# The transfers of a triangular substitution: from SP's queue, per chunk and block, to GpSimd's queue, per block for both chunks

## The chip, the cores and the metric

The kernel runs on one core of a Trainium2 chip. The metric is the device time of one execution in microseconds (us). Times of the profile count from the start of its span. PE is TensorE, with PEld its weight loads; DVE is VectorE, ACT is ScalarE, POOL is GpSimd and SP is SyncE, which here issues transfers only. SPq and POOLq are the instructions with which these engines issue transfers.

## The reference

A trunk of four pre-norm residual layers works on a sequence of 256 tokens of width 1024: a causal pooling mixer, a gated DeltaNet layer, an attention layer with compressed keys and values, and a pooling mixer again. All is fp32. The change lies in the second layer. Cut to what matters here:

```
proj = h @ w_in                       # q, k, v, gate, beta, decay
qkv = silu(causal_depthwise_conv(qkv, conv_w))
q, k = l2norm(q) * dk**-0.5, l2norm(k)          # 8 heads, dk 128, dv 256
L = where(strict, (k*beta) @ k.T * decay, 0)    # per head and chunk
A = eye(C) + L
sol = triangular_solve(A, [v*beta, k*beta*exp(g)], lower=True)
# then a scan over chunks: v_new = u - w @ state; o = q @ state + attn @ v_new; ...
y = rmsnorm(o) * silu(gate)
out = y.reshape(S, 2048) @ w_out
```

The reference takes chunks of 64 tokens. The kernel takes two chunks of 128, which gives the same output, and so needs the inverse of sixteen unit lower triangular matrices of 128 x 128 (8 heads, 2 chunks).

## The kernel before, in words

**Weights.** Every projection is made with split weights. `weights` (L115 to L130) loads a raw tile of 512 KB, two chunks of 128 rows and 512 columns, on SP's queue; for each chunk ACT rounds it to a high part `whi` (L128) and DVE subtracts that from the raw value for the low part `wlo` (L130). PE then makes three matmuls for each product: high by high, high by low, low by high. There are three raw buffers and nine of each of the parts (the ring). A raw buffer is free for the next load when the subtract of its second chunk has ended.

**Order.** The tile scheduler orders the instructions of all engines by a simulated timeline; what an engine then has in its order it executes in that order, and an instruction that waits holds all behind it on that engine. SP's transfers are such an order too. In the delta-rule layer (`gdn_layer`) PE's order is fixed as written: keys, queries, the gate and values are projected in 512-column pieces, and other steps of the layer are put between the k-chunks of a piece. `keys`, `queries` and `values` end in a convolution (`conv`: ACT scales, L658; DVE adds three taps, L661) and a SiLU on ACT (`kqT` L695, `vc` L816); PE then transposes `vc` (L100, `values_turned`) and ACT scales the result into `vR` (L829).

**The inverse.** `lower` writes `LT` on DVE (L721), one tile a chunk, with all heads. `substitution` (L746 to L779) inverts the 32 x 32 diagonal blocks, 64 in all (two chunks t, eight heads m, four blocks d). It brings them from `LT` to a layout with one block in each of 64 partitions by way of a DRAM buffer `d_l`: eight stores, one for each t and d (L752), and one load `Lb` (L757). On POOL it makes 31 steps of forward substitution (L762 product `pr`, L766 subtract into `Tb`). The result goes back by a buffer `d_t`: one store (L768) and eight loads into `T` (L772), again one for each t and d. All eighteen transfers are on SP's queue, among the raw loads. On POOL other work stands among the steps: the `Gb` product (L795), which needs the queries' `kqT`, and the norms `rq` (L797 to L801).

**What takes `T`.** `inverses` transposes `T` in blocks of 32 on DVE into `U` (L848) and clears parts of `Lb` and `Tb` on POOL (L847). `pairs`, `joined`, `turned`, `whole` and `last` are PE steps that assemble the whole inverse from the blocks; `pairs(0)`, 16 matmuls with `T` and `LT`, is the first of them. They stand in PE's fixed order among the k-chunks of `values(2)`, `values(3)` and `gate(3)`.

The order of the steps, as written (`scored` makes the attention tiles, `key_norms` and `query_norms` the norms):

```
queries(0, [do(lower, 0)], (), (), [do(key_norms, 1), do(lower, 1), substitution])
gate(1)
values(0, [do(query_norms, 0)], [do(scored, 0)])
queries(1, (), (), (), [do(values_turned, 0)])
gate(2)
values(1, [do(query_norms, 1)], [do(scored, 1)])
values(2, (), (), [do(values_turned, 1), inverses], [inv("pairs", 0)])
```

Of the kernel before, what the change touches and what calls it, by code (L numbers as in the profile page):

```python
# [16 lines left out]
P = 128  # L17
D = 1024
S = 256
NT = S // P  # L20
# [22 lines left out]
def trunk(ctx: ExitStack, tc: tile.TileContext, x, positions, norm_g, pool_w_in, pool_w_grp,  # L43
          pool_scale, pool_w_out, gdn_w_in, gdn_conv, gdn_a_log, gdn_dt_bias, gdn_norm_g,
          gdn_w_out, mla_w_in, mla_q_norm_g, mla_w_uq, mla_kv_norm_g, mla_w_ukv, mla_w_out,
          final_g, out, depth=4, final=True):
    nc = tc.nc
# [22 lines left out]
    def big(name, *dims, dt=F32):  # L70
        return s4.tile([P, *dims], dt, tag="s4", name=name)
# [7 lines left out]
    def small(name, *dims, bufs=2):  # L79
        return sm.tile([P, *dims], F32, tag=name, name=name, bufs=bufs)  # L80
# [14 lines left out]
    def matmul(*args, **opts):  # L95
        ins = nc.tensor.matmul(*args, **opts)  # L96
        return tc.keep_in_program_order(ins) if pinned["on"] else ins

    def transpose(*args):
        ins = nc.tensor.transpose(*args)  # L100
        return tc.keep_in_program_order(ins) if pinned["on"] else ins
# [460 lines left out]
    def gdn_layer(i, j, hT):  # L562
        H = GDN_H
# [71 lines left out]
        for t in range(NT):  # L635
            nc.gpsimd.dma_start(
                out=Gb[t].rearrange("p h s -> p (h s)"),
                in_=d_g[t * H:(t + 1) * H, :].rearrange("(a h) s -> a (h s)", a=1).to_broadcast(
                    [P, H * P]))
# [26 lines left out]
        Q, B = 4, 32  # L666
        Tb_ = big("Tb", B, B)
        Tb = Tb_[:M * Q]
        nc.gpsimd.memset(Tb, 0.0)
        nc.gpsimd.memset(Tb.rearrange("m r c -> m (r c)")[:, ::B + 1], 1.0)  # L670
        T = [big("T", H, P) for _ in range(NT)]
        for t in range(NT):
            nc.gpsimd.memset(T[t], 0.0)

# [37 lines left out]
        def against(dst, rhs, sf, hf, t):  # L712

            ps = bank(aux, "aux").rearrange("p (b s) -> p b s", b=4)
            tt = slice(t * P, (t + 1) * P)
            for b in range(4):
                matmul(ps[:, b], lhsT=kT[hf][:, b, tt], rhs=rhs[hf][:, b, tt],
                                 start=True, stop=True)
            for b in range(4):
                h = 4 * hf + b  # L720
                nc.vector.scalar_tensor_tensor(  # L721
                    out=dst[t][:, h, :], in0=ps[:, b], scalar=sf[:, t, h:h + 1],
                    in1=DT[t][:, h, :], op0=ALU.mult, op1=ALU.mult)

        LT = [big("LT", H, P) for _ in range(NT)]

        def keys(hf, *between):
            channels(kT, GDN_QK, hf, 0, between)
# [11 lines left out]
        def lower(hf):  # L740
            for t in range(NT):
                against(LT, kT, s2, hf, t)

        free = []

        def substitution():  # L746

            d_l = dram.tile([M * Q, B * B], F32, name="d_l")
            lv = d_l.rearrange("(t m d) (r c) -> t d r m c", t=NT, d=Q, r=B)
            for t in range(NT):  # L750
                for d in range(Q):
                    nc.sync.dma_start(out=lv[t, d],  # L752
                                      in_=LT[t][d * B:(d + 1) * B, :, d * B:(d + 1) * B])
            Lb_ = big("Lb", B, B)
            Lb = Lb_[:M * Q]
            free.extend((Lb_, Tb_))
            nc.sync.dma_start(out=Lb, in_=d_l.rearrange("m (r c) -> m r c", r=B))  # L757
            pr = small("pr", 256, bufs=1)[:M * Q]
            for r in range(B - 1):
                n, c = B - 1 - r, r + 1  # L760
                pv = pr[:, :n * c].rearrange("m (a b) -> m a b", a=n)
                nc.gpsimd.tensor_tensor(out=pv, op=ALU.mult,  # L762
                                        in0=Lb[:, r, r + 1:, None].to_broadcast([M * Q, n, c]),
                                        in1=Tb[:, r:r + 1, :c].to_broadcast([M * Q, n, c]))
                tv = Tb[:, r + 1:, :c]
                nc.gpsimd.tensor_tensor(out=tv, in0=tv, in1=pv, op=ALU.subtract)  # L766
            d_t = dram.tile([M * Q, B * B], F32, name="d_t")
            nc.sync.dma_start(out=d_t.rearrange("m (r c) -> m r c", r=B), in_=Tb)  # L768
            tv = d_t.rearrange("(t m d) (r c) -> t d r m c", t=NT, d=Q, r=B)
            for t in range(NT):  # L770
                for d in range(Q):
                    nc.sync.dma_start(out=T[t][d * B:(d + 1) * B, :, d * B:(d + 1) * B],  # L772
                                      in_=tv[t, d])
            nc.vector.reciprocal(rki, rk)
            nc.vector.tensor_tensor(out=kds, in0=rk[:, 0, :], in1=DT[0][:, :, P - 1],
                                    op=ALU.mult)
            nc.vector.tensor_scalar(neG, eG[:, 1, :], -1.0, None, ALU.mult)
            nc.gpsimd.tensor_tensor(out=ktok, in0=ktok, op=ALU.mult,
                                    in1=kds[:, :, None].to_broadcast([P, H, P]))  # L779
# [57 lines left out]
        def inverses():  # L837
# [8 lines left out]
            for t in range(NT):  # L846
                nc.gpsimd.memset(X1[t][:, :, 32:64], 0.0)  # L847
                nc.vector.transpose(U[t].rearrange("p m c -> p (m c)"),  # L848
                                    T[t].rearrange("p m c -> p (m c)"))

            def blocks(a, x):
                return a.rearrange("p m (a b c) -> p m a b c", a=2, b=2)[:, :, :, x]
# [3 lines left out]
            def pairs(t):  # L856
                ps = bank(aux, "aux").rearrange("p (m a c) -> p m a c", m=H, a=2)
                for h in range(H):
                    matmul(ps[:, h], lhsT=LT[t][:, h], rhs=blocks(T[t], 0)[:, h],
                           start=True, stop=True)  # L860
# [11 lines left out]
            def u_turned(t):  # L872
                ps = bank(aux, "aux").rearrange("p (m c) -> p m c", m=H)
                for h in range(H):
                    transpose(ps[:64, h], U[t][:64, h, :64], ident[:64, :64])
                nc.scalar.copy(T[t][:64, :, :64], ps[:64])

            def whole(t):
                ps = bank(aux, "aux").rearrange("p (m c) -> p m c", m=H)
                for h in range(H):  # L880
                    matmul(ps[:, h], lhsT=LT[t][:64, h], rhs=T[t][:64, h, :64],
                           start=True, stop=True)
# [179 lines left out]
    def mla_layer(i, j, hT):  # L1062
# [203 lines left out]
        return layer_out(mla_w_out[j], yT, units(POOL_W // P), i)  # L1266

    layers = (pool_layer, gdn_layer, mla_layer)
    setups = [gdn_setup, mla_setup][:max(0, depth - 1)]
    first = cols_of(pool_w_in[0], POOL_W + (len(WINDOWS) - 1) * CW)  # L1270
# [58 lines left out]
```

## Time and profile before

| | |
|---|---|
| median of 3 runs | 872.14 us (871.36 to 873.38) |
| profiled execution | 875.96 us |
| its span | 874.3 us |
| granted TensorE clock, mean | 0.979 |
| the delta-rule layer's stretch 215 to 345 us | PE waits 11.0 us for `vc`, 10.0 us for `kqT` |
| stretch 302 to 334 us | PE busy 21.03 of 32 us |

A row of a timeline has the start, the duration, the engine, the line and what it writes and reads, and in brackets how long the engine was idle before and what released it. A row of the waits has the waiting instruction, the one it waited for, the sum of us, the number of times and the longest. A row of transfers has the KB of one and the us from issue to landing. SP's rows of the timeline show only the issue, not the wait ahead of it.

### The profile page before, as it was taken

How to read it: one execution, taken by the hardware profiler on the slowest of the kernel's cores; microseconds unless marked ns; L12 is line 12 of the kernel's file. 1: busy time of each engine (PE TensorE's matmuls, PEld its weight loads, DVE VectorE, ACT ScalarE, POOL GpSimd, SP SyncE). 2: the span in 40 equal slices, each digit the busy share in tenths (PEclk: the TensorE clock that was granted, in tenths of full speed). 3: DMA queues.
4: the chain of work that ended last, by engine and by line, in shares of the span. 5: the costliest groups of instructions: out<-in, count | busy, mean ns of one | idle time of the engine just before them, and what ended most of it. 6: DMA issues, size and time to landing. Idle time of an engine off the chain costs nothing.

```text
span 874.3 us, 16119 instructions
## 1 busy us (share of the span) xinstructions
PE 839.3 (96%) x5967; PEld 782.2 (89%) x5967; DVE 597.6 (68%) x1142; ACT 490.3 (56%) x1006; POOL 150.2 (17%) x288
## 2 busy tenths in 40 slices
PE   7999999999779959999999999999999999999996
PEld 6999998989769949878988998999989989999986
DVE  5588776467868956556666667767867657767852
ACT  6566655466645534555556564556655566556542
POOL 4010000344119930012121101000000120000012
PEclk8999999999889988999999999999999999999999
DMA  7666656566455543213547776663453547566651
GB/s 237 205 193 194 189 171 218 147 183 204 121 145 150 165 124 108 82 49 121 166 124 209 216 167 169 180 183 97 136 153 98 168 141 218 179 189 193 195 192 49
DMA packets 111288, 140.43 MB, mean 161 GB/s; under 512 B 23340, under 2 KB 53224, under 8 KB 111208
## 3 DMA queue, kind: packets, MB, share of 16 engines
q1 hardware_dynamic: 109056, 138.17, 52.7%
q0 software_dynamic: 320, 1.06, 0.4%
q8 instruction: 47, 0.77, 0.3%
q10 hardware_dynamic: 1832, 0.16, 0.2%
q14 instruction: 33, 0.27, 0.1%
HBM read 137.79 MB, written 1.58 MB: 159 GB/s over the span
## 4 chain that ended last, share of the span: by engine, by line
PE 83%; POOL 7%; DMA 3%; DVE 3%; issue 1%; ACT 1%; SPq 0%; POOLq 0%; ACTq 0%; DVEq 0%
PE acc L96 68%; PE aux L96 12%; PE tp L100 3%; POOL Tb L766 3%; POOL pr L762 2%; DMA raw<-in_gdn_w_in_dram 2%; DMA gain<-in_norm_g_dram 1%; DVE h L329 1%; DVE wlo L130 1%; POOL xr L322 0%; ACT junk L235 0%; DMA Lb<-d_l 0%; POOL rq L683 0%; DVE x L379 0%; DVE cv L661 0%
## 5 line engine op out<-in xcount | busy, mean ns | idle before, releaser
L130 DVE TENSOR_TENSOR wlo<-raw,whi 128x512 fp32r<-128x512 f32 (+1 forms) x495 | 345.7, 719 | 175.0 <-ACT whi L128 168.3
L128 ACT CAST whi<-raw 128x512 fp32r<-128x512 f32 (+1 forms) x508 | 301.8, 618 | 278.9 <-PE acc L96 196.3
L96 PE MATMUL acc<-hTh,whi 128*128 128x256 f32 x832 | 236.3, 285 | 0.0
L96 PE MATMUL acc<-hTl,whi 128*128 128x256 f32 x832 | 235.7, 283 | 0.0
L96 PE MATMUL acc<-hTh,wlo 128*128 128x256 f32 x832 | 234.9, 282 | 0.0
L96 PEld LDWEIGHTS acc<-hTh,whi 128*128 128x128 f32 x832 | 158.4, 190 | 0.7
L96 PEld LDWEIGHTS acc<-hTl,whi 128*128 128x128 f32 x832 | 158.4, 190 | 0.4
L96 PEld LDWEIGHTS acc<-hTh,wlo 128*128 128x128 f32 x832 | 158.3, 190 | 0.1
L96 PE MATMUL acc<-whi,yTh 128*128 128x256 f32 (+1 forms) x384 | 116.7, 322 | 0.0
L96 PE MATMUL acc<-wlo,yTh 128*128 128x256 f32 (+1 forms) x384 | 116.5, 319 | 0.0
L96 PE MATMUL acc<-whi,yTl 128*128 128x256 f32 (+1 forms) x384 | 91.7, 318 | 0.0
L96 PEld LDWEIGHTS acc<-wlo,yTh 128*128 128x128 f32 x384 | 72.1, 188 | 5.0
L96 PEld LDWEIGHTS acc<-whi,yTh 128*128 128x128 f32 x384 | 71.9, 188 | 5.1
L96 PEld LDWEIGHTS acc<-whi,yTl 128*128 128x128 f32 x384 | 63.2, 188 | 5.8
L317 POOL TENSOR_TENSOR hg<-x,gain 128x256 f32<-128x256 f32 x18 | 14.9, 832 | 261.3 <-DVE x L379 256.8
L96 PE MATMUL acc<-whi,hTh 128*128 128x512 f32 (+1 forms) x144 | 56.9, 402 | 0.7 <-ACT hTh L221 0.7
L96 PE MATMUL acc<-wlo,hTh 128*128 128x512 f32 (+1 forms) x144 | 56.8, 397 | 0.5 <-DVE wlo L130 0.3
L96 PE MATMUL acc<-whi,hTl 128*128 128x512 f32 (+1 forms) x144 | 45.7, 390 | 0.0
L96 PEld LDWEIGHTS acc<-whi,hTh 128*128 128x128 f32 x144 | 27.8, 193 | 7.0 <-ACT hTh L221 1.9
L96 PEld LDWEIGHTS acc<-wlo,hTh 128*128 128x128 f32 x144 | 27.8, 193 | 7.0 <-DVE wlo L130 1.8
L461 POOL COPY win<-u 128x4 f32<-128x4 f32 x8 | 2.8, 355 | 175.7 <-ACT u L455 175.7
L96 PEld LDWEIGHTS acc<-whi,hTl 128*128 128x128 f32 x144 | 26.9, 190 | 5.6 <-DVE hTl L226 0.2
(336 smaller groups left out, 1423.2 us busy)
## 6 DMA issues: line engine op xcount, KB each, us to landing
raw<-in_pool_w_in_dram SPq DMA_DIRECT2D x60, 512.0 KB, 4.4
raw<-in_gdn_w_in_dram SPq DMA_DIRECT2D x48, 512.0 KB, 4.2
raw<-in_pool_w_out_dram SPq DMA_DIRECT2D x32, 512.0 KB, 3.7
raw<-in_mla_w_in_dram SPq DMA_DIRECT2D x24, 512.0 KB, 4.5
raw<-in_mla_w_uq_dram SPq DMA_DIRECT2D x36, 256.0 KB, 3.5
raw<-in_pool_w_grp_dram SPq DMA_DIRECT2D x16, 512.0 KB, 3.9
raw<-in_gdn_w_out_dram SPq DMA_DIRECT2D x16, 512.0 KB, 3.4
raw<-in_mla_w_ukv_dram SPq DMA_DIRECT2D x32, 256.0 KB, 3.1
```

The lines of the kernel that those rows point to most:

```text
L96: ins = nc.tensor.matmul(*args, **opts)
L100: ins = nc.tensor.transpose(*args)
L128: a = nc.scalar.copy(hi, v)
L130: b = e.tensor_tensor(out=lo, in0=v, in1=hi.bitcast(F32), op=ALU.subtract)
L317: nc.gpsimd.tensor_tensor(out=self.early[t, a], in0=xs[t][:, sl], in1=self.g[:, sl], op=ALU.mult)
L329: nc.vector.scalar_tensor_tensor(out=h[:, cut:], in0=xs[t][:, sl], scalar=r[:, 0:1], in1=self.g[:, sl], op0=ALU.mult, op1=ALU.mult)
L461: nc.gpsimd.tensor_copy(nxt[:, :, :d], cur[:, :, :d])
L762: nc.gpsimd.tensor_tensor(out=pv, op=ALU.mult, in0=Lb[:, r, r + 1:, None].to_broadcast([M * Q, n, c]), in1=Tb[:, r:r + 1, :c].to_broadcast ...
L766: nc.gpsimd.tensor_tensor(out=tv, in0=tv, in1=pv, op=ALU.subtract)
```

## The change

The eighteen transfers of `substitution` are issued by POOL, not SP. `LT` and `T` become one tile each for both chunks, and the rows of `d_l` and `d_t` are ordered so that one transfer takes a diagonal block d of all heads and both chunks: four stores, `Lb`, `d_t` and four loads, ten in all. Each store or load of a block now moves 32 partitions by 16 runs of 32 numbers (64 KB), where it was 32 by 8 (32 KB). The arithmetic is the same.

```diff
-        T = [big("T", H, P) for _ in range(NT)]
+        Ts = big("T", NT, H, P)
+        T = [Ts[:, t] for t in range(NT)]
+
+        def diagonal(a, d):
+
+            return a[d * B:(d + 1) * B, :, :, d * B:(d + 1) * B].rearrange("p t h c -> p (t h) c")
+
...
-        LT = [big("LT", H, P) for _ in range(NT)]
+        LTs = big("LT", NT, H, P)
+        LT = [LTs[:, t] for t in range(NT)]
...
             d_l = dram.tile([M * Q, B * B], F32, name="d_l")
-            lv = d_l.rearrange("(t m d) (r c) -> t d r m c", t=NT, d=Q, r=B)
-            for t in range(NT):
-                for d in range(Q):
-                    nc.sync.dma_start(out=lv[t, d],
-                                      in_=LT[t][d * B:(d + 1) * B, :, d * B:(d + 1) * B])
+            lv = d_l.rearrange("(m d) (r c) -> d r m c", d=Q, r=B)
+            for d in range(Q):
+                nc.gpsimd.dma_start(out=lv[d], in_=diagonal(LTs, d))
...
-            nc.sync.dma_start(out=Lb, in_=d_l.rearrange("m (r c) -> m r c", r=B))
+            nc.gpsimd.dma_start(out=Lb, in_=d_l.rearrange("m (r c) -> m r c", r=B))
...
             d_t = dram.tile([M * Q, B * B], F32, name="d_t")
-            nc.sync.dma_start(out=d_t.rearrange("m (r c) -> m r c", r=B), in_=Tb)
-            tv = d_t.rearrange("(t m d) (r c) -> t d r m c", t=NT, d=Q, r=B)
-            for t in range(NT):
-                for d in range(Q):
-                    nc.sync.dma_start(out=T[t][d * B:(d + 1) * B, :, d * B:(d + 1) * B],
-                                      in_=tv[t, d])
+            nc.gpsimd.dma_start(out=d_t.rearrange("m (r c) -> m r c", r=B), in_=Tb)
+            tv = d_t.rearrange("(m d) (r c) -> d r m c", d=Q, r=B)
+            for d in range(Q):
+                nc.gpsimd.dma_start(out=diagonal(Ts, d), in_=tv[d])
```

Lines behind the first piece have other numbers in the changed kernel: the stores of `LT` are L758, `Lb` L762, the steps L767 and L771, `d_t` L773, the loads of `T` L776, the `Gb` product L798, the memset of `Tb` L850.

SP's queue in the delta-rule layer, from the middle of the raw loads of the input projection to those of the output projection (rows with - are of before, with + of the change):

```order
-L757 DMA Lb<-d_l 64x1024
-L115 DMA raw<-in_gdn_w_in_dram 128x2x512 x13
-L768 DMA d_t<-Tb 64x1024
-L115 DMA raw<-in_gdn_w_in_dram 128x2x512
-L772 DMA T<-d_t 32x8x32 x5
-L115 DMA raw<-in_gdn_w_in_dram 128x2x512
-L772 DMA T<-d_t 32x8x32 x3
-L115 DMA raw<-in_gdn_w_in_dram 128x2x512 x5
+L115 DMA raw<-in_gdn_w_in_dram 128x2x512 x48
 L115 DMA raw<-in_gdn_w_out_dram 128x2x512 x8
```

Before, three single raw loads stood behind `d_t` and between the loads of `T`; now the 48 raw loads follow each other with nothing between them.

POOL's order in the same layer at the start of the substitution, before (`ktok` is the scaled keys, the row ahead of `Gb`):

```order
L778 TENSOR_TENSOR ktok<-ktok,kds 128x1024
L795 TENSOR_TENSOR Gb<-Gb,kqT 128x512
L762 TENSOR_TENSOR pr<-Lb,Tb 64x31
L766 TENSOR_TENSOR Tb<-Tb,pr 64x31
L762 TENSOR_TENSOR pr<-Lb,Tb 64x60
```

and now, the same place:

```order
L781 TENSOR_TENSOR ktok<-ktok,kds 128x1024
L758 DMA d_l<-LT 32x16x32 x4
L762 DMA Lb<-d_l 64x1024
L798 TENSOR_TENSOR Gb<-Gb,kqT 128x512
L767 TENSOR_TENSOR pr<-Lb,Tb 64x31
L771 TENSOR_TENSOR Tb<-Tb,pr 64x31
```

The four stores and the load of `Lb` have come between `ktok` and the `Gb` product; the steps follow as before. At the end of the substitution POOL's order has, in the change:

```order
L767 TENSOR_TENSOR pr<-Lb,Tb 64x31
L804 TENSOR_SCALAR rq_2525<-rq_2525 128x2x4
L771 TENSOR_TENSOR Tb<-Tb,pr 64x31
L773 DMA d_t<-Tb 64x1024
L776 DMA T<-d_t 32x16x32 x4
L850 MEMSET Tb 128x8x32
```

where before the memset stood right behind the last subtract. `d_t` and the four loads of `T` have moved in ahead of it.

The scheduler also moves work at the start of the program. PE's order in the first layer, at the end of the first 12 matmuls (`hTh_168` and `hTl_169` are the high and low parts of the transposed input for the first four k-chunks, `hTh_177` and `hTl_178` for the last four):

```order
 L96 MATMUL acc<-whi,hTl_169 128x512
+L100 MATMUL tp<-ident,h 128x128 x8
 L96 MATMUL acc<-whi,hTh_177 128x512
+L96 MATMUL acc<-whi,hTh_168 128x512
+L96 MATMUL acc<-wlo,hTh_168 128x512
 L96 MATMUL acc<-wlo,hTh_177 128x512
```

The transposes of the second half of the tokens of `h` now follow 12 matmuls and followed 22 before. On ACT two pairs of `whi` casts, which stood around the squares of that half of the tokens, now stand behind its `h` (L334).

## The prediction

> **What bounds the kernel now.** I read the chain that ended last first, then busy time by stretch, then the waits of the delta-rule layer, and last the timelines of its queues.
>
> ```profile
> PE 83%; POOL 7%; DMA 3%; DVE 3%; issue 1%; ACT 1%; SPq 0%; POOLq 0%; ACTq 0%; DVEq 0%
> 302.00:334.00 32.00, 21.03 (x156) 20.44 (x155) 17.43 (x34) 11.38 (x24) 10.99 (x23) 0.79 0.41 115
> 334.00:420.00 86.00, 85.12 (x534) 74.31 (x534) 52.37 (x107) 46.46 (x114) 10.72 (x32) 1.00 0.28 92
> 420.00:874.00 454.00, 446.55 (x3243) 418.61 (x3242) 310.75 (x595) 254.45 (x542) 39.21 (x70) 1.00 0.56 164
> ```
>
> In the three rows by stretch the columns are the stretch, its length, then busy time of PE, PEld, DVE, ACT and POOL, the granted clock, the DMA share and GB/s. The kernel is bound by PE, which is full from 334 us to the end (85.12 of 86, 446.55 of 454). What comes earlier at 334 us therefore comes earlier at the end, nearly one for one. Between 302 and 334 us PE is idle 11 us, and that is the place where the change works. Who waits for whom there, from the waits:
>
> ```profile
> PE tp L100 <- ACT vc L816: 11.0, 2, 8.6
> PE tp L100 <- ACT kqT L695: 10.0, 3, 5.4
> SPq L768 <- POOL Tb L766: 11.7, 1, 11.7
> ```
>
> PE waits 11.0 us for two `vc` activations of ACT, and SP's queue stands 11.7 us at the store of `d_t` (L768), because POOL has not finished the substitution. The timelines, SP, POOL, ACT, DVE and PE, join the two (start, duration, instruction, and in brackets the idle time before it and its releaser):
>
> ```profile
> 313.54 0.24 POOL L766 TENSOR_TENSOR Tb<-Tb,pr 64x31 f32<-64x31 f32 x1
> 313.81 0.46 SPq L768 DMA_DIRECT2D d_t<-Tb  x1
> 314.36 0.54 SPq L115 DMA_DIRECT2D raw<-in_gdn_w_in_dram  x1
> 316.76 2.30 SPq L772 DMA_DIRECT2D T<-d_t  x5
> 319.15 0.40 SPq L115 DMA_DIRECT2D raw<-in_gdn_w_in_dram  x1
> 321.15 1.29 SPq L115 DMA_DIRECT2D raw<-in_gdn_w_in_dram  x2
> 318.90 1.14 ACT L128 CAST whi<-raw 128x512 fp32r<-128x512 f32 x2 [9.24 <-DMA raw<-in_gdn_w_in_dram]
> 323.59 0.62 ACT L128 CAST whi<-raw 128x512 fp32r<-128x512 f32 x1 [3.54 <-DMA raw<-in_gdn_w_in_dram]
> 324.11 0.63 ACT L816 ACTIVATE vc<-vc 128x512 f32<-128x512 f32 x1
> 326.37 0.62 ACT L128 CAST whi<-raw 128x512 fp32r<-128x512 f32 x1 [1.12 <-DMA raw<-in_gdn_w_in_dram]
> 326.89 0.83 ACT L829 ACTIVATE vR<-tp,rki 128x256 f32<-128x256 f32 x2
> 327.62 0.63 ACT L816 ACTIVATE vc<-vc 128x512 f32<-128x512 f32 x1
> 306.86 0.85 DVE L130 TENSOR_TENSOR wlo<-raw,whi 128x512 fp32r<-128x512 f32 x1 [0.54 <-ACT whi L128]
> 310.59 0.68 DVE L130 TENSOR_TENSOR wlo<-raw,whi 128x512 fp32r<-128x512 f32 x1
> 326.28 2.36 DVE L848 STREAM_TRANSPOSE U<-T 128x1024 f32<-128x1024 f32 x2
> 324.79 1.11 PE L100 MATMUL tp<-ident,vc 128*128 128x128 f32 x4 [8.57 <-ACT vc L816]
> 328.30 1.11 PE L100 MATMUL tp<-ident,vc 128*128 128x128 f32 x4 [2.39 <-ACT vc L816]
> 333.93 1.73 PE aux L96 x16
> ```
>
> Three weight loads stand in SP's queue behind `d_t`. The buffers of the second and the third are free when the subtracts at 306.86 and 310.59 end, at 307.7 and 311.3; they go out at 319.15 and 321.15. ACT's casts wait for them, the `vc` activations stand behind those casts in ACT's order, and PE's transposes wait for `vc`. The last row, from the chain, is `pairs(0)`, the first work of PE that needs `T`.
>
> **The change, part by part.** It has three: the wait leaves SP; POOL issues the transfers; they are fewer. The order of other work moves a little besides.
>
> *SP freed.* All 48 loads of the input projection now follow each other on SP, each at the moment its buffer is free. The second load goes out at 307.7 and lands in about 4.5 us (before: 314.36 to the cast that it released at 318.90), at 312.2. Its cast (0.62) and `vc` (0.63) are then done near 314, where ACT and DVE still have their own order to keep. PE comes to the first transposes at 324.79 − 8.57 = 316.2. So that wait goes whole: 8.57 us. The third load leaves at 311.3 and is there at 315.8, ahead of the end of the first transposes at 317.3. Then the second `vc` hangs on the first transposes alone: ACT starts `vR` when they end and takes up `vc` behind it, and from the start of `vR` (326.89) to the second transposes (328.30) are 1.41 us. Of the 2.39 us, 0.98 go. PE would be at `pairs(0)` 8.57 + 0.98 = 9.55 us earlier, at 324.4. Bounds: 0, if something else is as late, and 10.96, if both waits go.
>
> *Is `T` there by 324.4?* This is what the rest hangs on. Rows of POOL, its older transfers, `LT` on DVE, and the transfers' landing times (KB, then us from issue to landing):
>
> ```profile
> 247.19 2.15 DVE L721 SCALAR_TENSOR_TENSOR LT<-aux,s,DT 128x128 f32<-128x128 f32 x8
> 257.67 1.27 POOL L795 TENSOR_TENSOR Gb<-Gb,kqT 128x512 f32<-128x512 f32 x1 [12.41 <-ACT kqT L695]
> 261.36 0.23 POOL L762 TENSOR_TENSOR pr<-Lb,Tb 64x31 f32<-64x31 f32 x1 [2.42 <-DMA Lb<-d_l]
> 204.32 0.80 POOL L633 DMA_DIRECT2D d_g<-grow  x1
> 207.41 1.09 POOL L636 DMA_DIRECT2D Gb<-d_g  x2 [2.29 <-DMA d_g<-grow]
> raw<-in_gdn_w_in_dram SPq DMA_DIRECT2D x48, 512.0 KB, 4.2
> Gb<-d_g POOLq DMA_DIRECT2D x2, 512.0 KB, 5.9
> d_l<-LT SPq DMA_DIRECT2D x8, 32.0 KB, 1.7
> Lb<-d_l SPq DMA_DIRECT2D x1, 256.0 KB, 3.6
> d_t<-Tb SPq DMA_DIRECT2D x1, 256.0 KB, 2.9
> T<-d_t SPq DMA_DIRECT2D x8, 32.0 KB, 3.4
> d_g<-grow POOLq DMA_DIRECT2D x1, 8.0 KB, 2.8
> ```
>
> POOL's issue of one transfer took 0.80 us (16 rows of `d_g`) and 1.09 / 2 = 0.55 us (128 rows of `Gb`): it did not grow with the rows. The new ones move 32 x 16 = 512 short runs each, which no row shows. If the issue did grow with the pieces from `Gb` on, it would be 4 x 0.55 = 2.2 us. I take 0.7, between the two rows, since eight times the rows cost no more there, and keep 0.55 and 2.2 as ends.
>
> A rule of the Trainium skill ("SBUF — State Buffer", A bandwidth-pool intuition that's wrong) speaks against the change: a GpSimd-issued transfer that takes about 620 ns alone takes about 3100 ns beside a VectorE copy, since its descriptors wait for a port that VectorE holds. By it, with 3.1 us an issue, the sum would be an estimated +6 us; by the rows it is the one below. The `Gb` rows speak against it, for DVE was at work beside them, but not with these operations alone.
>
> The landing: `d_g` on POOL took 2.8 us for 8 KB, `d_l` on SP 1.7 us for 32 KB, so 1.1 us more; `Gb` took 1.7 us more than the raw tiles of its size. I take 1.1 and keep 0 and 1.7.
>
> The chain then: `LT` is done at 247.19 + 2.15 = 249.3, which all four stores now wait for, since each holds both chunks. The fourth is issued 3 x 0.7 later, at 251.4, and lands at 251.4 + 1.7 + 1.1 = 254.2. `Lb` takes 3.6 + 1.1 and lands at 258.9. The `Gb` product stands between in POOL's order; it hangs on `kqT` and ends at 258.94 as before, so it is no later. The substitution starts at 259.0, 2.4 us ahead of 261.36, and takes its 313.78 − 261.36 = 52.4 us: the end is at 311.4. `d_t` lands 4.0 later, at 315.4; the second `T` load at 315.4 + 0.7 + 4.5 = 320.6, the fourth at 322.0. `pairs(0)` waits for two of the four, so it has 3.8 us to spare, 2.4 if it were for all. Eight issue times stand on this chain (ten for the fourth load), so nothing is lost up to 0.7 + 3.8 / 8 = 1.2 us an issue, and the gain is used up at 0.7 + (333.9 − 320.6) / 8 = 2.4 us.
>
> Who stands behind the new waits: on POOL, `Lb` waits for the stores with the `Gb` product behind it, and `T` waits for `d_t` with the memset of `Tb` behind it, which came after that landing before too. On DVE `U` (L848) takes all four loads. DVE would reach it 9.55 us earlier, at 316.7, and stand there to 322.0; `U` is over at 324.4 where it was at 328.6. That there are eight stores and loads instead of sixteen frees only issue time of SP, which had nothing else to do: nothing.
>
> *Other work moved.* In the 220s a cast stands one earlier in ACT's order and frees a buffer some half a cast (0.62) earlier, ahead of a wait of PE for `kqT`: −0.3 us (0 to −0.6). At the start of the program the order of SP, ACT and PE moves:
>
> ```profile
> 11.53 7.15 PE acc L96 x22
> 18.68 0.87 PE tp L100 x8
> 17.18 0.91 ACT L334 ACTIVATE h<-hg,xr 128x256 f32<-128x256 f32 x2 [0.67 <-POOL xr L322]
> ```
>
> The second group of transposes now comes after 12 matmuls, so at 11.53 + 12 x 7.15 / 22 = 15.4, and needs an `h` that ended at 18.1. Its half of the tokens of `x` is now loaded two raw tiles earlier, and four casts of ACT leave its path. If two to four of them (0.62 each) are saved, that `h` ends at 15.6 to 16.9: PE waits 0.2 to 1.5 us, and I take +0.6.
>
> **Sum.** −9.55 − 0.3 + 0.6 = −9.25 us. Against the profiled execution's own 875.96 us (span 874.3) that is 866.7; the median of the runs is 872.14, 3.8 us below that execution, and 872.14 − 9.25 = **862.9 us**. A measurement of this kernel can tell about 0.2%, 1.7 us, from no change.
>
> **The rivals.**
>
> *DVE stands at `U` too long* (0.2). The loads land some us later (the upper landing cost, four landings at +0.6, and 1.0 us an issue give 320.6 + 2.4 + 2.4 = 325.4), and behind `U` the subtracts for PE's next chunks are late: the fourth load at 327.4, `U` at 329.8, the next subtract (0.68) at 330.4. Against it speaks that the ring holds nine chunks, with PE behind the oldest. PE loses 1 to 6 of its 9.25 us: 864 to 869.
>
> *The issue grows with pieces* (0.06): at 2.2 us the second load lands at 320.6 + 8 x 1.5 = 332.6, the gain is 1.3 us, and with the start 0.6 the time is 871 to 872, no change. For it: 512 pieces are four times `Gb`'s. Against: the two rows.
>
> *POOL is held up while it writes its transfers, and the kernel is slower* (0.09). DVE goes on with its subtracts right behind `LT`, while POOL issues the stores. Should each issue take 3 us, `T` lands at 320.6 + 8 x 2.3 = 339.0, and PE, with nothing else to do in its fixed order, gets to `pairs(0)` 5.1 us later than now: 877.2. It decides from 2.4 us. Against: the two `Gb` issues took 0.55 us each with DVE at work. The rule of the Trainium skill quoted above ("SBUF — State Buffer") is one way in which that could come about; the stores of `LT` would meet another mix of VectorE work than `Gb` did.
>
> *More than forecast* (0.07): both `vc` waits go whole and the start costs nothing, −10.96 − 0.6: 860.6.
>
> **Numbers.** The forecast has 0.58. Faster: 0.58 + 0.2 + 0.07 = 0.85; same 0.06; slower 0.09. The range of 8 in 10 is from 860.5 to 869.0.
>
> **What would show it.** In the profile after, SP should have no wait for POOL and ACT no 9 us wait for a raw load near 310; PE's first wait for `vc` should be gone and `pairs(0)` begin near 324.4; each POOL issue in L758 and L776 should be near 0.7 us, `Lb` should land near 259 and the last `T` near 322; DVE should stand at `U` for about 5 us. I am wrong if PE waits for `T`, if the POOL issues take over 1.2 us, or if PE's wait for weights comes back behind `U`.

## The result and the profile after

The changed kernel takes 865.05 us (median of 4 runs, 863.53 to 866.88), the kernel before 872.76 us beside it (4 runs): a ratio of 0.9914, 95% interval 0.989 to 0.9939. The gain is 7.7 us, where 9.25 were forecast. The profiled execution of the change took 864.45 us (span 862.6), close to its median; that of before was 3.2 us above its own. The two spans therefore differ by 11.7 us, and some 4 us of that is one execution and not the change.

SP's queue after, from 297 to 326 us, the stretch in which it stood at `d_t` before, has one row, seven raw loads and nothing else:

```profile
297.09 29.29 SPq L115 DMA_DIRECT2D raw<-in_gdn_w_in_dram  x7
```

The waits of PE after that bear on this, in the whole kernel (waiting instruction, what it waited for, sum, times, longest):

```profile
PE tp L100 <- ACT kqT L701: 8.0, 3, 5.7
PE tp L100 <- DVE h L329: 3.5, 2, 1.8
PE aux L96 <- DMA T<-d_t: 2.8, 1, 2.8
PE tp L100 <- ACT vc L819: 1.4, 1, 1.4
```

The 11.0 us for `vc` are 1.4, as worked out: what is left is the second `vc` behind `vR`. In its place stands a new wait, 2.8 us for `T`. The PE timeline around it, and the same kernel's POOL and DVE:

```profile
312.82 0.60 PE L100 MATMUL tp<-ident,vc 128*128 128x128 f32 x4
314.87 0.66 PE L100 MATMUL tp<-ident,vc 128*128 128x128 f32 x4 [1.45 <-ACT vc L819]
321.11 2.53 PE L96 MATMUL aux<-T,LT 128*128 128x64 f32 x16 [2.75 <-DMA T<-d_t]
246.86 2.71 POOL L758 DMA_DIRECT2D d_l<-LT  x4 [4.37 <-DVE LT L727]
254.26 0.56 POOL L762 DMA_DIRECT2D Lb<-d_l  x1 [4.70 <-ACT kqT L701]
257.65 0.23 POOL L767 TENSOR_TENSOR pr<-Lb,Tb 64x31 f32<-64x31 f32 x1 [1.42 <-DMA Lb<-d_l]
312.04 0.25 POOL L771 TENSOR_TENSOR Tb<-Tb,pr 64x31 f32<-64x31 f32 x1
312.59 0.65 POOL L773 DMA_DIRECT2D d_t<-Tb  x1 [0.29 <-POOL Tb L771]
317.93 2.62 POOL L776 DMA_DIRECT2D T<-d_t  x4 [4.69 <-DMA d_t<-Tb]
322.44 2.37 DVE L851 STREAM_TRANSPOSE U<-T 128x1024 f32<-128x1024 f32 x2 [9.20 <-DMA T<-d_t]
248.07 1.88 DVE L130 TENSOR_TENSOR wlo<-raw,whi 128x512 fp32r<-128x512 f32 x3
```

PE comes to `pairs(0)` at 321.11 − 2.75 = 318.4 and finds no `T`. The bracket at `Lb` names a `kqT` row of ACT; by the program `Lb` waits for the four stores alone, and the slowest of these took 5.0 us to land. The transfers of POOL landed, by the page (medians):

```profile
d_l<-LT POOLq DMA_DIRECT2D x4, 64.0 KB, 4.6
Lb<-d_l POOLq DMA_DIRECT2D x1, 256.0 KB, 3.3
d_t<-Tb POOLq DMA_DIRECT2D x1, 256.0 KB, 5.0
T<-d_t POOLq DMA_DIRECT2D x4, 64.0 KB, 2.4
```

The issue of one 64 KB transfer took 2.71 / 4 = 0.68 and 2.62 / 4 = 0.66 us, against 0.7 taken. DVE was at its subtracts beside the stores of `LT` (248.07) and held none of them up; beside the loads of `T` it stood idle. So the rule of the Trainium skill on descriptors that wait for VectorE ("SBUF — State Buffer", A bandwidth-pool intuition that's wrong) does not show here, with VectorE at two-input subtracts and multiply-adds. That rule is told of a VectorE copy, which did not run beside these stores, and its 3100 ns are those of a whole transfer; the estimate of +6 us ahead of the result took them for the issue alone.

A second thing is seen only in the granted clock. In the kernel before, by 4 us slices (stretch, length, busy PE, PEld, DVE, ACT, POOL, clock, DMA share, GB/s):

```profile
318.00:322.00 4.00, 0.00 (x0) 0.00 (x0) 2.44 (x5) 1.14 (x2) 0.00 (x0) 0.68 0.62 137
322.00:326.00 4.00, 1.11 (x4) 0.71 (x4) 1.78 (x5) 1.66 (x3) 0.00 (x0) 0.50 0.92 284
326.00:330.00 4.00, 1.70 (x8) 1.70 (x9) 3.22 (x4) 2.42 (x6) 0.00 (x0) 0.50 0.53 168
330.00:334.00 4.00, 4.00 (x25) 4.00 (x24) 0.69 (x1) 1.65 (x5) 0.00 (x0) 0.62 0.00 0
```

After PE's long wait the clock is at half. By slices of 1 us it is back at full only at 333 us, 8 us after PE went on, with the second wait of 2.39 us in between. So work that no longer waits is slow: four transposes took 1.11 us there and 0.60 to 0.66 in the change, and the 24 matmuls ahead of `pairs(0)` took 4.52 us (329.42 to 333.93) where the change needed 318.36 − 315.53 = 2.83. These waits of PE cost their length and something more behind them. The change pays this too, on a smaller scale, after its wait for `T`:

```profile
322.00:326.00 4.00, 4.00 (x23) 4.00 (x23) 3.56 (x5) 0.00 (x0) 0.00 (x0) 0.57 0.00 0
326.00:330.00 4.00, 4.00 (x38) 4.00 (x37) 4.00 (x9) 1.24 (x2) 0.00 (x0) 1.00 0.48 135
```

`pairs(0)` took 2.53 us, where the second such step took 1.73, and the 24 matmuls behind it 3.90 where the next 24 took 2.89: 1.8 us in all. The drop came behind the wait, not in it: by slices of 1 us the clock was 1.00 up to 322 us, when PE had been at work again since 321.11, and then 0.67, 0.50, 0.50 and 0.63.

### The profile page after: what moved, and what is told of

Same layout as the page of the kernel before. It is cut to its first block, busy times and chain, and to the rows that moved or that the text cites. A ratio compares the mean times of both kernels' runs of the same rounds, so it can differ in the third digit from the quotient of the medians.

```text
span 862.6 us, 16114 instructions
## 1 busy us (share of the span) xinstructions
PE 836.6 (97%) x5967; PEld 779.3 (90%) x5967; DVE 594.7 (69%) x1142; ACT 489.3 (57%) x1006; POOL 160.1 (19%) x298
## 4 chain that ended last, share of the span: by engine, by line
PE 79%; POOL 8%; DMA 4%; DVE 4%; ACT 2%; issue 2%; SPq 0%; POOLq 0%; ACTq 0%; DVEq 0%
PE acc L96 65%; PE aux L96 12%; POOL Tb L771 3%; PE tp L100 3%; POOL pr L767 3%; DMA raw<-in_gdn_w_in_dram 1%; DMA raw<-in_pool_w_in_dram 1%; DVE wlo L130 1%; DMA Gb<-d_g 1%; DVE h L329 1%; DVE cv L661 1%; ACT junk L235 1%; DMA d_t<-Tb 1%; POOL xr L322 1%; DVE DT L643 0%
```

## The experiments

My theory after the result: the gain comes from SP no longer standing at `d_t`; what is left of the forecast is lost to PE's wait for `T` and the low clock behind it. Rivals: that fewer and larger transfers did it; that the front half (the stores of `LT`) took part; that the wait for `T` has something as late right behind it. All ratios below are to the kernel before on the same chip, with a 95% interval.

**The merged transfers on SP.** All four issuing lines go back to SP, the merging stays:

```diff
-                nc.gpsimd.dma_start(out=lv[d], in_=diagonal(LTs, d))
+                nc.sync.dma_start(out=lv[d], in_=diagonal(LTs, d))
...
-            nc.gpsimd.dma_start(out=d_t.rearrange("m (r c) -> m r c", r=B), in_=Tb)
+            nc.sync.dma_start(out=d_t.rearrange("m (r c) -> m r c", r=B), in_=Tb)
```

(and `Lb` and `T` likewise.)

> The merged transfers of the change (four stores, four loads), all still on SP's queue. Theory (the gain comes from SP no longer standing at d_t): SP waits about 11 us for POOL again, PE waits about 8 us for the first vc, and the time is 871 to 873, as before. Rival (fewer and larger transfers are what helped): PE's wait for vc is mostly gone on SP too, 865 to 868.

871.02 us, ratio 0.9977 (0.9965 to 0.9989). SP again issues `d_t` only when POOL is done, and PE waits:

```profile
298.84 0.37 SPq L115 DMA_DIRECT2D raw<-in_gdn_w_in_dram  x1
310.31 0.46 SPq L773 DMA_DIRECT2D d_t<-Tb  x1
310.87 0.57 SPq L115 DMA_DIRECT2D raw<-in_gdn_w_in_dram  x1
313.26 1.39 SPq L776 DMA_DIRECT2D T<-d_t  x3
314.75 0.43 SPq L115 DMA_DIRECT2D raw<-in_gdn_w_in_dram  x1
320.47 1.12 PE L100 MATMUL tp<-ident,vc 128*128 128x128 f32 x4 [5.76 <-ACT vc L819]
```

The theory's case: SP stands at `d_t` again, and of the 7.7 us about 2 come without the new queue. The wait of 5.76 us is shorter than the 8.57 of before. Three loads of `T` stand ahead of the second raw load here and five did before; in the run with only the front half on POOL, below, it is four, and the wait is 7.36. The wait follows their number, though that was not tried by itself.

**The small transfers on POOL.** Before's `LT`, `T` and sixteen transfers, with `nc.gpsimd` for `nc.sync` in all of `substitution`.

> The sixteen small transfers of before, d_l, Lb, d_t and T all issued by POOL. Theory (each issue on POOL takes 0.65 us and T is what PE waits for now): four more stores and at least one more load ahead of what pairs(0) needs make T 3 to 4 us later, PE waits about 6 us for T, time 868 to 870. Rival (the stores land late because of the raw loads beside them, so their number does not matter): 865 to 866.

870.01 us, ratio 0.9958 (0.9942 to 0.9974), over 12 runs that lie apart: from 865.99 to 873.16. The profiled execution is one of the short ones (866.08); PE waited 4.1 us for `T` in it, `Lb` went out at 255.77, where the change had it at 254.26, and eight stores took 4.74 us of POOL. On this queue the merging is worth some 5 us by the medians, at the end of the range that the theory gave. In the profiled execution, though, it was about 1 us, with 1.3 us more of PE's wait than in the change, where some 3 had been expected. The runs of 870 us and more had a granted clock of 0.981 to 0.984, the three shortest 0.988 to 0.990; what the longer ones wait for was not profiled, so this part of the theory is not shown.

**Only the back half on POOL, only the front half on POOL.** The merged transfers, split over the two queues (`d_t` and `T` on POOL, or `LT`'s stores and `Lb`).

```diff
-                nc.gpsimd.dma_start(out=lv[d], in_=diagonal(LTs, d))
+                nc.sync.dma_start(out=lv[d], in_=diagonal(LTs, d))
```

(the first of the two, with `Lb` likewise; in the second it is `d_t` and `T` that go to `nc.sync`.)

> Merged transfers; the stores of LT and Lb on SP, d_t and T on POOL. Theory (the gain is all in the back half, where SP stood at d_t): 863 to 866, as the change. Rival (the front half costs too: the raw loads behind Lb's wait on SP are late and PE waits longer for kqT): 867 to 869.

864.43 us, ratio 0.9913 (0.9891 to 0.9935): all of the gain.

> Merged transfers; the stores of LT and Lb on POOL, d_t and T on SP. Theory: SP stands at d_t as before, PE waits 8 us or more for vc, 870 to 873. Rival (the front half carries a part of the gain): 867 to 869.

873.25 us, ratio 1.0 (0.9985 to 1.0014): none of it, and just above the range expected. Its PE waits nearly as before:

```profile
314.08 1.94 SPq L776 DMA_DIRECT2D T<-d_t  x4
321.87 1.12 PE L100 MATMUL tp<-ident,vc 128*128 128x128 f32 x4 [7.36 <-ACT vc L819]
324.43 1.12 PE L100 MATMUL tp<-ident,vc 128*128 128x128 f32 x4 [1.45 <-ACT vc L819]
```

Together they settle the place: it is `d_t` and `T`, and moving the stores of `LT` and `Lb` brings nothing. Whether `d_t` alone would do, with the loads of `T` left on SP, was not tried.

**T earlier.** In the change POOL does other work between the steps of the substitution. Here the query norms stand behind the issue of `d_t` and the second `Gb` product behind the loads of `T` (`later(x)` keeps what stands in it behind instruction x in the order; `mark["dt"]` is the issue of `d_t`, `mark["tl"]` the last load of `T`; the lines that go from the old place are not shown):

```diff
+            with later(mark["dt"]):
+                nc.gpsimd.tensor_scalar(qh, ssq[:, 1, :, 4 * hf:4 * hf + 4], float(P), EPS * P,
+                                        ALU.mult, ALU.add)
+                power(rh, qh)
...
+            with later(*[mark["tl"]] if hf else []):
+                nc.gpsimd.tensor_tensor(out=ev, in0=ev, in1=qT[hf][:, :, P:], op=ALU.mult)
```

> The change, and POOL does the query norms (two chains of four small operations) behind the issue of d_t and the second Gb product behind the loads of T, so that the substitution is not held up by them. Theory (T is what PE waits for, and POOL's own other work of about 7 us stands ahead of it): T lands 5 us or more earlier, PE's wait of 2.8 us for T goes, and the half-speed clock behind it too: 860 to 861.5. Rival (something else is as late as T there, such as weights): 864 to 865.

861.97 us, ratio 0.9888 (0.9869 to 0.9906). `d_t` goes out 6 us earlier, part of the norms stand in the time in which POOL waits for it to land, and PE has no wait for `T` left:

```profile
306.54 0.59 POOL L773 DMA_DIRECT2D d_t<-Tb  x1 [0.29 <-POOL Tb L771]
307.49 1.67 POOL L689 TENSOR_TENSOR rq<-rq,halves 128x8 f32<-128x8 f32 x1
310.24 2.69 POOL L776 DMA_DIRECT2D T<-d_t  x4 [0.80 <-DMA d_t<-Tb]
319.34 1.90 PE L96 MATMUL aux<-T,LT 128*128 128x64 f32 x16
```

`pairs(0)` takes 1.90 us, without a wait. By the medians the gain over the change is 3 us, just short of what was expected. The profiled execution itself took 864.26 us at a granted clock of 0.937, where the other four had 0.987 to 0.991; it is read here for its order and waits, not its length. The moved `Gb` product has a price: beside it (312.95 to 314.24) a subtract of DVE ahead of the second `vc` took 1.80 us, where its neighbours took some 0.65, and PE's wait for that `vc` was 1.70 us instead of 1.45.

**T later.** Six multiplications of `Tb` by 1.0 on POOL ahead of `d_t`.

```diff
+            for _ in range(6):
+                nc.gpsimd.tensor_scalar(Tb, Tb, 1.0, None, ALU.mult)
```

> The change with six multiplications of Tb by 1.0 on POOL ahead of d_t, about 6 us of it. Theory: T lands 6 us later and PE, with nothing else in its order, waits 6 us longer: 871 to 872.5. Rival (T has slack, the wait is only shown there): 865 to 867.

881.72 us, ratio 1.0101 (1.0082 to 1.0119). My price of the added work was wrong: the six took 17.35 us, not 6. PE's wait for `T` grew from 2.8 to 18.2 us, by 15.4, and the time by 16.7 us over the change: about one for one, and no slack.

```profile
315.04 17.35 POOL L773 TENSOR_SCALAR Tb<-Tb 64x1024 f32<-64x1024 f32 x6
PE aux L96 <- DMA T<-d_t: 18.2, 1, 18.2
```

**The waits filled.** To test the clock, matmuls whose result is not used were put on PE in the place of a wait: twelve ahead of `pairs(0)` in the change, forty ahead of the transposes of `vc` in the kernel before.

```diff
+                if t == 0:
+                    idle = bank(aux, "aux")
+                    for _ in range(12):
+                        matmul(idle[:, :S], lhsT=kT[0][:, 0, :P], rhs=kT[0][:, 1, :], start=True, stop=True)
```

> The change with twelve matmuls whose result is not used ahead of pairs(0), about 12 x 0.22 = 2.6 us, in the place of PE's wait of 2.8 us for T. Theory (the wait costs more than its length since the granted clock is about half for some us after it): pairs(0) and the group behind it run at full clock, 1.8 us less than the change: 863 to 863.5. Rival (the clock drop is not caused by the wait): 865 or, with the added matmuls, 865 to 866.

> The kernel before with forty matmuls whose result is not used ahead of the transposes that wait 8.6 us for vc, about 40 x 0.22 = 8.6 us. Theory of the clock: the work from those transposes to pairs(0) runs at full clock, 3 to 4 us less than before: 869 to 870. Rival: 872 to 873.5.

873.73 us, ratio 1.0008 (0.9991 to 1.0026), and 877.42 us, ratio 1.0054 (1.0039 to 1.007). Both missed, because one such matmul took 0.43 us, twice my price: the forty took 17.27 us where the wait was 8.6 (the rows count two instructions for each). Even so the first shows the clock at 1.00 up to 330 us, and `pairs(0)` behind the added work took 1.89 us, not 2.53. But there was more in it: the scheduler laid DVE's order out anew, with more taps of the next convolution ahead of the masks of `pairs(0)`, and PE waited 4.9 us for those taps, which DVE could only begin when it was through with `U`. That is close to the first rival of the prediction, with taps in the place of subtracts: work of DVE that stands behind `U` can make PE wait.

```profile
318.65 5.34 PE L96 MATMUL aux<-kqT 128*128 128x256 f32 x24
323.22 2.37 DVE L851 STREAM_TRANSPOSE U<-T 128x1024 f32<-128x1024 f32 x2 [9.54 <-DMA T<-d_t]
327.68 4.50 DVE L661 SCALAR_TENSOR_TENSOR vc<-acc,tap,vc 128x254 f32<-128x254 f32 x11
331.41 0.55 PE L96 MATMUL acc<-hTh,whi 128*128 128x256 f32 x1 [4.92 <-DVE vc L661]
```

The second was made again with nineteen.

> The kernel before with nineteen added matmuls, not forty, ahead of the transposes that wait for vc; one took 17.27 / 40 = 0.43 us in the run with forty, so 8.2 us, just less than PE's wait of 8.6 us there. Theory of the clock (work after a long wait runs at about half clock): from the first of these transposes to pairs(0) PE needs about 3 us less, 869 to 870. Rival (nothing comes of it): 872 to 873.5.

870.83 us, ratio 0.998 (0.9967 to 0.9993): 1.7 us less than before, with useless work added; that lies between the two ranges expected, 869 to 870 and 872 to 873.5. The transposes take 0.65 us instead of 1.11, and the 24 matmuls behind the second of them 2.84 instead of 4.52:

```profile
312.27 8.36 PE L96 MATMUL aux<-kqT 128*128 128x256 f32 x38
320.87 0.65 PE L100 MATMUL tp<-ident,vc 128*128 128x128 f32 x4 [0.24 <-ACT vc L816]
323.45 0.66 PE L100 MATMUL tp<-ident,vc 128*128 128x128 f32 x4 [1.93 <-ACT vc L816]
324.11 2.84 PE acc L96 x24
```

The granted clock is 1.00 throughout, from 310 to 335 us. So the low clock is caused by the wait. The size by the profile is 2 x 0.45 + 1.7 = 2.6 us; by the medians 1.7.

**The late norms with the front half on SP, and the change again.** Run together on one chip.

> The late norms together with the stores of LT and Lb on SP, d_t and T on POOL. T is then ahead of PE by several us either way. Theory (T's place no longer matters once PE does not wait for it): as the late norms alone, 861 to 862.5. Rival (the front on SP frees POOL for more): 860 or less.

> The change itself, unaltered, beside the other two on one chip: 864 to 866, with which the late norms are compared.

862.92 us, ratio 0.9885 (0.9868 to 0.9903), and 865.45 us, ratio 0.9916 (0.9895 to 0.9936). In the first, just above its range, PE has no wait for `T`; with `T` ahead of PE, the queue of the front half no longer matters within 1 us. The subtract beside the moved `Gb` product took 2.05 us in it, PE's wait for the second `vc` was 1.94 us, and the 24 matmuls behind that wait took 4.36 us where the change needed 2.83: the product, moved to this place, brings a low clock back. In the profiled execution of the second, at 867.32 us, PE waits 3.6 us for `T`: the wait comes again. By the medians the late norms, alone or with this, are 2.5 to 3.5 us faster than the change. On this chip the five runs of the first lie below the six of the change, 863.50 at most against 863.59 at least, but the intervals of the late norms and of the change overlap a little.

## Why the prediction was right

The place, the sign and the mechanism were right, and the time lies in the range. One of the forecast's own signs of being wrong did come, PE's wait for `T`, and two terms were missing that partly cancel; that the sum came within 1.6 us of the measured gain owes something to luck.

*SP freed* held: the forecast was 9.55 us of PE's wait for `vc`, and 11.0 became 1.4, which is 9.6, with the second `vc` as described. The two halves tried apart show that all of it lies at `d_t` and `T`.

*Is `T` there by then* failed as a step: 3.8 us to spare were forecast, and PE waited 2.75. The load that PE needed landed at 320.98 against 320.6 forecast (the second load, 2.4 us behind its issue at 318.62), so the forecast of that moment was nearly exact; but by offsets. The first store went out 2.5 us earlier. Against that, it took 7.4 us from there to `Lb`'s issue (254.26 − 246.86), not 4.9, since up to 5.0 us to landing and not 2.8 is what the stores took; the substitution took 312.29 − 257.65 = 54.6 us, not 52.4; `d_t` took 5.35 us from the end of the substitution, not 4.0. `Lb` and `T` were 1.3 and 1.9 us quicker than priced. My price of the landing came from rows of POOL transfers at other places; in the run with the delay `d_t` took 2.96 us with no raw load issued near it, where it took 5.05 beside two raw loads in the change, so its neighbours have a part in it, as the two runs suggest. In the kernel before, on SP, it took 2.9 us with one raw load issued 0.55 us behind it, so a part of the queue or of the order is not ruled out.

What was earlier was PE: it came to `pairs(0)` at 318.4, not 324.4. Of the 6.0 us, 2.7 were there at the transposes of the second `kqT` (254.01 instead of 256.73), and 0.7 came on the way from these to the first `vc`: the low clock behind that wait for `kqT` ended 3.5 us after PE went on, where it took 4.6 before. The other 2.6 are the clock behind the waits for `vc`, which the sum did not have at all (0.5 and 0.45 us of the two groups of transposes, 1.7 of the 24 matmuls). The sum missed two terms of opposite sign: the clock that comes back with the waits gone, some −2.6 us by the profile, and the wait for `T` with its own low clock, 2.75 + 1.8 = +4.55 us. −9.25 with these two is −7.3; −7.7 was measured.

*Other work moved.* The start cost about what was forecast: 0.6, measured 0.53 between these two executions. These are the same transposes of the first layer before and after:

```profile
69.60 0.22 PE tp L100 x2
```

```profile
70.13 0.22 PE tp L100 x2
```

(The change run again has them at 69.58, the two kernels of before with added matmuls at 68.89 and 69.02, so single executions differ as much as the term is large.)

In the 220s the profile shows more than the 0.3 us forecast: PE's wait there fell from 3.97 to 1.50 us. I do not count it to the change, since the two profiles of the kernel before with added matmuls had 8.2 and 8.5 us of waits for `kqT` in all, where the profiled execution of before had 10.0 and the change has 8.0; what is left for the change is a few tenths.

*The rivals.* Issue growing with the pieces is out: 0.66 to 0.68 us for 512 runs, 0.59 for 256 (4.74 / 8). POOL held up by DVE did not come, beside subtracts. DVE at `U` did come, 9.2 us instead of 5, but PE lost nothing to weights by it in the change; in the filled run it lost 4.9 us, to taps.

## What to carry to other kernels

A queue that executes in order should not hold a transfer that waits for a long computation ahead of transfers that others wait for; moving that one transfer (here `d_t` with its loads) is the whole gain here, and what stands before it in the same chain can stay. When a wait goes, the next latest input can take its place, as `T` did, so look for other work that stands ahead of that input on the engine that makes it: here some 7 us of small operations on POOL that nobody needed yet (without them the substitution took 47.0 us from its first product to its last subtract, and 54.6 with them). And price a wait of PE with what comes after it: behind all the waits of 2.6 us and more above, work ran at the low clock for some microseconds.

## What the runs showed of the hardware

- PE's granted clock went to half behind a wait of 2.75 us (`pairs(0)` at 2.53 us instead of 1.73 to 1.90), and did not behind one of 1.45 us (transposes at 0.66 us). Between these it went either way: behind 1.94 us it fell (the late norms with the front half on SP), behind 1.93 us it did not (the kernel before with nineteen added matmuls). Filling an 8.6 us wait with 8.36 us of matmuls kept it up.
- A POOL issue took 0.59 us for 256 runs of 128 bytes, 0.66 to 0.68 for 512, 0.56 for the 64 rows of `Lb`: nearly a constant.
- A multiplication of 64 x 1024 fp32 by a constant took POOL 17.35 / 6 = 2.9 us, though a memset of that size took 0.98.
